# Weight sums on GpSimd and its own DMA queue, and a down projection that begins beside the third chunk, in a streaming encoder layer

## The chip, the cores and the metric

One core of a Trainium2 chip runs the whole layer in one launch. The metric is the device time of one execution in microseconds (us), and a kernel's time is the median of its timed runs. The engines of the core are named as in the profile: PE is TensorE, DVE is VectorE, ACT is ScalarE, POOL is GpSimd, SP is SyncE, which in this kernel only issues DMAs.

## The reference, cut to what matters

One layer (DEPTH 1, D 1024) acts on 1024 prompt frames and 32 sample frames, 1056 tokens that share the weights.

```python
h = rms_norm(x, g_mix); z = h @ w_in
q, k, v, ch, cb, cc, ga, gb = jnp.split(z, SPLITS, axis=-1)
a = attn_core(q, k, v) @ w_attn_out      # 16 heads of 64, window of 128, sink
u = cc * ch                              # then a causal convolution of width 3 over the frames
bo = (cb * conv) @ w_conv_out
x = x + (jax.nn.sigmoid(ga) * a + jax.nn.sigmoid(gb) * bo) @ w_mix_out
x = x + co @ w_co                        # co: cross-attention into 256 memory tokens
hm = rms_norm(x, g_mlp)
x = x + jnp.square(jax.nn.relu(hm @ w_up)) @ w_down   # w_up 1024 x 4096, w_down 4096 x 1024
```

A final RMSNorm gives the outputs. All is float32.

## The kernel before, in words

**Tiling.** Activations lie with their features on the 128 partitions and their tokens along the free dimension, in three chunks of 384, 384 and 288 tokens (`CH`), the last 32 of which are the sample. A feature block is 128 features, so x has 8 blocks of each chunk. A product of float32 is made of three matmuls in fp32r: each operand x is split into hi (a rounded copy) and lo = x - hi, and hi·hi, hi·lo and lo·hi are accumulated (`gemm` L166 to L173, `part` L1358 to L1365, `product` L1084 to L1086).

**Weights** come in tiles of 128x1024 (512 KB). `fetch_w` (L131) issues the load on SP's queue into one of two `wr` tiles. `issue_w` (L136) splits it: ScalarE copies to `wh` (L119), VectorE subtracts into `wl` (L120), three buffers each. `next_w` keeps two weights split ahead of the one in use. The list `plan` holds the kernel's steps with their weights, and `run` emits them; within each engine a scheduler at build time then orders the instructions by its own estimates, and each engine works in that order. An instruction whose operand isn't there holds up all that stands behind it on its engine; this is also so on SP's queue, whose DMA instructions wait for the tile that they store or overwrite.

**The stages,** with the times of the profile: the first norm, K and V (to about 100 us); the attention in 36 units (`Unit`), each beside a "host", a projection for Q, for the convolution or a gate (to about 560); the gates 3 to 7, the attention's output projection, and the second half of the gates (560 to 865); convolution output, mixing and cross-attention, chunk by chunk (to 1236); the up projection (to 1505); the down projection (to 1850); and the last norm of chunk 1.

**One attention unit** (`scores` L492) makes its scores on TensorE; GpSimd copies the negated sinks into the last column of the score tile `S` (L517); VectorE finds the negated maximum `nmx` (L521); ScalarE takes the exponentials over scores and sink column together, with their sum (L526); VectorE inverts that and scales (L532); `turn` transposes on TensorE (L540). GpSimd's other work there is a part of the convolution: products at L578, L591 and L593 and small copies.

**The weight sums.** The up and down projections on chunks 0 and 1 go by a scheme of seven products on 2x2 blocks (Strassen's, in Winograd's form) instead of eight. For the down projection it needs, beside the four quarters w0 to w3 of w_down, four sums of quarters: w2+w3, w0+w2, w0+(the first), w1+(that). `sum_step` (L733 to L749) makes them in 32 pieces, each with 256 columns of all four quarters, 512 KB: load, four VectorE adds of 128x256 (L736 to L739), store to `wsum_d` in DRAM. One piece takes two steps, and a host of three chunks has three steps (`steps3`), from gate 3 on. Even pieces use a tile `ws` of 128x4x256 with one DMA each way; odd ones use four separate tiles (`acc0` to `acc2` and `wsx`) with four DMAs each way. So 160 DMAs are issued on SP.

**Up** (`up_pair` L1131) makes a pair of feature blocks of the 4096 with seven products for chunks 0 and 1, and chunk 2 plainly. Twelve pairs cover three quarters of the blocks; the first eight blocks are done plainly earlier. Their values for the down projection are stored by `hidden` (L983) as operands b11, b12, b21, b22, and the combinations n3, n1, t2, n4 of four of them each are made pair by pair. For the blocks that were done plainly the combinations have to be made afterwards: `refold` (L1004) loads four blocks of 128x384, subtracts four times on VectorE (L1013 to L1016) and stores four; that is done four times, during the pairs 2 to 5.

**Down** runs eight stages (`stages` L1430). Each has eight weight tiles; a weight serves one block of eight 384-column operands (24 matmuls) and, in the first four stages, also chunk 2 (`two`, 24 more of 288 columns). The first stage has only chunk 2. Operands are loaded and split by `load_op` and `load_h2` within one step: the split stands right behind the load. The order of the products is chunk 2 alone with w_down 2, then n4 (w_down 3), b21 (w_down 1), b11 (w_down 0), t2, n3, n1, b22 with the sums; n3 goes on in t2's accumulator, and b22 in n1's.

## Time and profile before

| | |
|---|---|
| time, median of 3 runs | 1867.37 us (1866.73 to 1873.9) |
| the profiled execution | 1866.89 us, span 1865.1 us |
| busy in the span: PE, DVE, ACT, POOL | 1783.8 (96%), 1141.1 (61%), 756.6 (41%), 393.6 us (21%) |
| matmuls | 11172 |
| mean granted clock of PE | 0.983 |
| moved by DMA | 293.36 MB, 157 GB/s on average |

The profile is of one execution. A group's row gives, after a bar, the busy time, the mean of one instruction in ns, and the idle time of the engine just before them, with what ended most of it. An instruction's row in order of time gives its start, its duration, the engine, the line, the operation, and in brackets how long the engine stood idle before it and for what. A row of the waits gives the waiter, the releaser, the sum in us, how often, and the longest. A row of the DMA issues gives the queue, how many, the size of each, and the median time in us from issue to landing. A busy PE is not always at full speed: the granted clock says how much of it the chip allowed in a stretch.

### The profile page before, as it was taken

Reading aid. Unit: us, or ns where it says so; the run is one execution under the profiler, and the core shown is the slowest. Engines: PE = TensorE matmul, PEld = TensorE weight load, DVE = VectorE, ACT = ScalarE, POOL = GpSimd, SP = SyncE. Lnnn points to the kernel's source line nnn. Section 1 sums busy time; section 2 is a strip of 40 time slices with the busy share of each in tenths; the row PEclk is TensorE's granted clock in tenths of the full one; section 3 lists DMA queues with packets and bytes.
Section 4 is the critical chain, followed back from the end, with each engine's and each line's share of the span. In section 5 each row is a group of like instructions: output and inputs, shape, how many; then the busy total and the mean of one; then the engine's idle time right before and its main releaser. Section 6 shows DMA issues by size and latency. Waiting matters only on the chain. (4 is left out here: it accounts for less than half of the span.)

```text
span 1865.1 us, 30056 instructions
## 1 busy us (share of the span) xinstructions
PE 1783.8 (96%) x11172; PEld 1759.0 (94%) x11172; DVE 1141.1 (61%) x2203; ACT 756.6 (41%) x1486; POOL 393.6 (21%) x405
## 2 busy tenths in 40 slices
PE   7999999999999787899999989999999989999997
PEld 7999999999999787899999989998999989999997
DVE  7766767757656443434666677776776564445664
ACT  7643435334344100223455655642222253333453
POOL 3211010201100000001424142275455400001011
PEclk9999999999999998999999989999999999999998
DMA  4411111212238777614765657764554385444673
GB/s 182 138 64 57 61 55 60 73 51 70 69 95 250 202 231 225 215 62 133 238 239 184 227 199 251 240 212 158 177 172 132 115 272 171 167 134 147 205 248 113
DMA packets 167842, 293.36 MB, mean 157 GB/s; under 512 B 18160, under 2 KB 129552, under 8 KB 167568
## 3 DMA queue, kind: packets, MB, share of 16 engines
q1 hardware_dynamic: 167696, 291.44, 48.4%
q8 instruction: 88, 1.44, 0.3%
q14 instruction: 58, 0.48, 0.1%
HBM read 217.89 MB, written 73.48 MB: 156 GB/s over the span
## 5 line engine op out<-in xcount | busy, mean ns | idle before, releaser
L171 PE MATMUL acc<-X,wh 128*128 128x384 f32 (+1 forms) x1200 | 391.9, 327 | 16.6 <-DVE Gb L621 8.1
L172 PE MATMUL acc<-X,wh 128*128 128x384 f32 (+1 forms) x1200 | 388.4, 324 | 1.5 <-DVE X L246 1.5
L173 PE MATMUL acc<-X,wl 128*128 128x384 f32 (+1 forms) x1200 | 387.3, 323 | 0.2 <-DVE wl L120 0.2
L119 ACT CAST wh<-wr 128x1024 fp32r<-128x1024 f32 x208 | 218.2, 1049 | 405.4 <-PE acc L172 208.9
L120 DVE TENSOR_TENSOR wl<-wr,wh 128x1024 fp32r<-128x1024 f32 x208 | 276.6, 1330 | 115.4 <-ACT wh L119 114.3
L171 PEld LDWEIGHTS acc<-X,wh 128*128 128x128 f32 x1200 | 226.7, 189 | 19.0 <-ACT wh L119 7.0
L171 PE MATMUL acc<-Y,wh 128*128 128x384 f32 (+1 forms) x624 | 207.2, 332 | 26.7 <-DVE ct L706 20.9
L172 PEld LDWEIGHTS acc<-X,wh 128*128 128x128 f32 x1200 | 227.3, 189 | 2.8 <-DVE X L246 2.2
L173 PEld LDWEIGHTS acc<-X,wl 128*128 128x128 f32 x1200 | 227.1, 189 | 0.8 <-DVE wl L120 0.8
L173 PE MATMUL acc<-Y,wl 128*128 128x384 f32 (+1 forms) x624 | 205.1, 329 | 1.0 <-DMA wl<-wl_d 1.0
L172 PE MATMUL acc<-Y,wh 128*128 128x384 f32 (+1 forms) x624 | 205.0, 329 | 0.0
L171 PEld LDWEIGHTS acc<-Y,wh 128*128 128x128 f32 x624 | 120.0, 193 | 31.3 <-DVE ct L706 15.6
L242 POOL TENSOR_TENSOR xacc<-xacc,ct 128x384 f32<-128x384 f32 (+1 forms) x62 | 78.9, 1274 | 317.9 <-ACT ct L240 312.6
L173 PEld LDWEIGHTS acc<-Y,wl 128*128 128x128 f32 x624 | 120.2, 193 | 1.2 <-DMA wl<-wl_d 1.2
L172 PEld LDWEIGHTS acc<-Y,wh 128*128 128x128 f32 x624 | 120.1, 192 | 0.0
L1363 PE MATMUL acc<-Y,wh 128*128 128x384 f32 (+1 forms) x352 | 113.8, 323 | 2.2 <-ACT wh L119 2.2
L1365 PE MATMUL acc<-Y,wl 128*128 128x384 f32 (+1 forms) x352 | 113.8, 323 | 1.4 <-DVE wl L120 1.4
L1364 PE MATMUL acc<-Y,wh 128*128 128x384 f32 (+1 forms) x352 | 113.7, 323 | 0.0
L796 POOL TENSOR_TENSOR ct<-ct,ct 128x384 f32<-128x384 f32 (+1 forms) x21 | 26.9, 1283 | 408.6 <-DVE ct L795 369.4
L119 ACT CAST PTh<-pt 128x512 fp32r<-128x512 f32 (+3 forms) x94 | 46.3, 517 | 129.8 <-PE pt L540 122.3
L120 DVE TENSOR_TENSOR Y<-ct,Y 128x384 fp32r<-128x384 f32 (+1 forms) x128 | 65.8, 547 | 27.6 <-ACT Y L119 27.4
L119 ACT CAST Y<-ct 128x384 fp32r<-128x384 f32 (+1 forms) x128 | 58.3, 486 | 50.1 <-DMA ct<-ao_d 13.8
(314 smaller groups left out, 4112.7 us busy)
## 6 DMA issues: line engine op xcount, KB each, us to landing
wr<-in_w_in SPq DMA_DIRECT2D x50, 512.0 KB, 3.3
wr<-in_w_up SPq DMA_DIRECT2D x48, 512.0 KB, 4.4
wr<-in_w_down SPq DMA_DIRECT2D x32, 512.0 KB, 3.4
wr<-wsum_d SPq DMA_DIRECT2D x32, 512.0 KB, 3.8
wl<-wl_d SPq DMA_DIRECT2D x28, 512.0 KB, 4.6
wr<-in_w_conv_out SPq DMA_DIRECT2D x24, 512.0 KB, 4.2
wr<-in_w_mix SPq DMA_DIRECT2D x24, 512.0 KB, 4.4
ct<-b_d SPq DMA_DIRECT2D x64, 192.0 KB, 4.1
```

The costliest lines, as they stand in the source:

```text
L119: act.copy(hi, src)
L120: dve.tensor_sub(lo, src, hi.bitcast(F32))
L171: pe.matmul(out, wh[:, a], hi, start=(k == 0), stop=False)
L172: pe.matmul(out, wh[:, a], lo, start=False, stop=False)
L173: pe.matmul(out, wl[:, a], hi, start=False, stop=(k == len(acts) - 1))
L242: pool_e.tensor_tensor(acc, acc, sq, op=ALU.add)
L796: (dve if f == NF - 1 else pool_e).tensor_tensor(t, t, t1, op=ALU.add)
L1363: pe.matmul(a, wh[:, s], hi, start=(start and k == 0), stop=False, skip_group_check=True)
L1364: pe.matmul(a, wh[:, s], lo, start=False, stop=False, skip_group_check=True)
L1365: pe.matmul(a, wl[:, s], hi, start=False, stop=(stop and k == len(acts) - 1), skip_group_check=True)
```

## The change

1. **Weight sums.** The adds and the DMAs of a piece are GpSimd instructions: `pool_e.dma_start` issues them on GpSimd's own queue, and `pool_e.tensor_tensor` adds. `w_down` and `wsum_d` are laid out so that a piece is contiguous (rows of 4 KB in each partition); in return a weight tile of the down projection is read in four rows of 1 KB for each partition. A new tile `xacc` of 128x1056 takes the place of `acc0` to `acc2` and `wsx`: the odd pieces use it whole, the sums of squares use its three parts, and the up stage's `r` lies in it too. One step now loads the next piece and then finishes the one before (four adds, a store), and a host has two steps.
2. **Stores later.** `hidden` and the stores of n3, t2, n1, n4 in `up_pair` go through `put` into a list, and `flush` issues that list one product later.
3. **Refold moved.** The four refolds leave the up stage and stand in the first stage of down, in tiles of their own (`fold`).
4. **Another order of down.** It begins with b11 and w_down 0 beside chunk 2, then b21 (w_down 1), n4 (w_down 3), t2 with w_sum 0, whose steps alternate with chunk 2's rest (w_down 2), then n3, n1, b22. n3 starts an accumulator of its own, so t2's is added to x1 by itself, with the opposite sign for one block: eight more VectorE adds.
5. **Loads a step ahead.** `pump(n)` first splits what the last call loaded and then issues the next n loads; `pace` spreads them over a stage.

The diff, cut:

```diff
-    wsum_d = dram.tile([4, 4, 2, P, 1024], F32, name="wsum_d")
+    wsum_d = dram.tile([4, 2, 4, P, 4, 256], F32, name="wsum_d")
...
+        if name in ("w_down", "w_sum"):
+            q, j, t = at
+            return (wsum_d if name == "w_sum" else io[name])[j, t, :, :, q].rearrange("i p c -> p i c")
...
+    def xacc_tile():
+        xacc[0] = tp.tile([P, 1056], F32, tag="xacc", name=nm("xacc"))
+        return xacc[0]
...
-            accs[c] = [tp.tile([P, n], F32, tag=f"acc{c}", name=nm("xacc"))]
+            accs[c] = [xacc[0][:, CH[c][0] : CH[c][0] + n]]
...
+    def sum_tile(n):
         if n % 2:
-            new = [tp.tile([P, CH[c][1]], F32, tag=f"acc{c}", name=nm("ws"))[:, :256] for c in range(3)]
-            return None, new + [W["pool"].tile([P, 256], F32, tag="wsx", name=nm("wsx"))]
+            return xacc_tile()[:, :1024].rearrange("p (q c) -> p q c", q=4)
+        return W["pool"].tile([P, 4, 256], F32, tag="ws", name=nm("ws"))
...
     def sum_step():
-        if "new" in W:
-            at, all4, t = W.pop("new")
-            dve.tensor_add(t[3], t[2], t[3])
-            dve.tensor_add(t[2], t[0], t[2])
-            dve.tensor_add(t[0], t[0], t[3])
-            dve.tensor_add(t[1], t[1], t[0])
-            W["made"] = at, all4, t
-            return
-        if "made" in W:
-            at, all4, t = W.pop("made")
-            sum_dma(False, all4, t, quarters(wsum_d, *at))
+        old = W.pop("new", None)
         if pieces:
             at = pieces.pop(0)
-            all4, t = sum_tiles(len(pieces))
-            sum_dma(True, all4, t, quarters(io["w_down"], *at))
-            W["new"] = at, all4, t
-    steps3 = [(c, sum_step) for c in range(3)]
+            t = sum_tile(len(pieces))
+            pool_e.dma_start(t, io["w_down"][at])
+            W["new"] = at, t
+        if old:
+            at, t = old
+            for to, x, y in ((3, 2, 3), (2, 0, 2), (0, 0, 3), (1, 1, 0)):
+                pool_e.tensor_tensor(t[:, to], t[:, x], t[:, y], op=ALU.add)
+            pool_e.dma_start(wsum_d[at], t)
+    steps3 = [(c, sum_step) for c in (0, 2)]
...
+    def put(*args):
+        later.append(args)
+    def flush():
+        for args in later:
+            sp.dma_start(*args)
+        later.clear()
     def hidden(c, j, h):
-        sp.dma_start(hid2_d[:, half, i] if c == 2 else op_d[f"b{half + 1}{c + 1}"][:, i], h)
+        put(hid2_d[:, half, i] if c == 2 else op_d[f"b{half + 1}{c + 1}"][:, i], h)
...
+    def pump(n):
+        for into, at, t, get in coming:
+            into[at] = (get(), get())
+            split(*into[at], t)
+        coming.clear()
+        for into, at, src, cols, get in wanted[:n]:
+            t = tmp(cols)
+            sp.dma_start(t, src)
+            coming.append((into, at, t, get))
+        del wanted[:n]
...
+    def refold(step):
+        if step % 2 == 0:
+            if fold:
+                for to, k in (("n3", "b22"), ("n1", "b12"), ("t2", "b11"), ("n4", "b21")):
+                    sp.dma_start(op_d[to][:, step // 2 - 1], fold[k])
+            if step < 8:
+                for k in ("b12", "b22", "b11", "b21"):
+                    fold[k] = H["pool"].tile([P, 384], F32, tag="fold", bufs=4, name=nm("fold"))
+                    sp.dma_start(fold[k], op_d[k][:, step // 2])
+        else:
+            for to, x, y in (("b22", "b12", "b22"), ("b12", "b11", "b12"), ("b11", "b11", "b22"), ("b21", "b21", "b11")):
+                dve.tensor_sub(fold[to], fold[x], fold[y])
...
+    def beside_two(w, kind, then, half, f, begin, more=(), each=None):
...
+            def fn(ws, j=j, t=t, n=n):
+                prod(kind, j, t, then)(ws)
+                pump(pace(13 - 2 * n))
+                if each:
+                    each(n)
+                two(half, j, t, f, begin)(ws)
+                pump(pace(12 - 2 * n))
+            item(fn, ("w_down", w, j, t))
...
+    want(twos(0, 1), ops("b21"))
+    beside_two(0, "b11", ((*C12, True, False), (*C21, False, False), (*C22, False, False), (*C11, True, False)), 0, 0, True,
+               twos(1, 0), refold)
+    item(lambda: refold(8))
+    want(twos(1, 1), ops("n4"))
+    beside_two(1, "b21", ((*C11, True, True),), 1, 0, False)
+    want(ops("t2"))
+    beside_two(3, "n4", ((*C21, True, False),), 1, 4, True, twos(0, 0))
...
```

**Where the instructions stand.** Three places, as the builds of before and of the change order them. A row is an instruction with its line, its output and inputs, the shape, and in brackets the counters it waits for; an xN at the end stands for equal rows that follow each other.

GpSimd in the attention, between the sink copies of two neighbouring units; `Ga` are convolution products, `R` the row of norms. Before:

```order
L517 COPY S_1824<-nsink 128x4 [waits DVE_49,PE_49,Activation_49]
L578 TENSOR_TENSOR Ga_297_1729<-Ga_297_1729,R_390 128x384 [waits DVE_49]
L578 TENSOR_TENSOR Ga_299_1757<-Ga_299_1757,R_594 128x384 [waits DVE_49]
L517 COPY S_1970<-nsink 128x4 [waits PE_49,Activation_49]
L578 TENSOR_TENSOR Ga_307_1803<-Ga_307_1803,R_786 128x288 [waits DVE_49]
```

With the change, from the same copy on (`in_w_down` is the weight in DRAM, and the lines have moved by ten):

```order
L527 COPY S_1824<-nsink 128x4 [waits DVE_49,PE_49,Activation_49]
L745 DMA wsum_d<-xacc_7567 128x1024 [waits Pool_49]
L739 DMA xacc_7671<-in_w_down 128x1024 [waits DMASW3_49]
L744 TENSOR_TENSOR xacc_7671<-xacc_7671 128x256 [waits DMASW4_49]
L744 TENSOR_TENSOR xacc_7671<-xacc_7671 128x256 [waits Pool_49] x3
L588 TENSOR_TENSOR Ga_297_1729<-Ga_297_1729,R_390 128x384 [waits DVE_49]
L745 DMA wsum_d<-xacc_7671 128x1024 [waits Pool_49]
L588 TENSOR_TENSOR Ga_299_1757<-Ga_299_1757,R_594 128x384 [waits DVE_49]
L527 COPY S_1970<-nsink 128x4 [waits PE_49,Activation_49]
L739 DMA xacc_7775<-in_w_down 128x1024 [waits DMASW5_49]
L588 TENSOR_TENSOR Ga_307_1803<-Ga_307_1803,R_786 128x288 [waits DVE_49]
```

All 16 pieces that use `xacc` now stand in the first part of GpSimd's program, between its first instruction and the sink copy of the tenth unit; the 16 pieces that use `ws` stand behind the attention, where their pool is opened. The next piece's load waits for the store of the one before, since they share the tile.

SP among the attention output's weights. Before:

```order
L133 DMA wr_6890<-in_w_attn_out 128x1024
L731 DMA wsum_d<-wsx_7068 128x256
L731 DMA wsum_d<-ws_7067 128x256
L731 DMA wsum_d<-ws_6984 128x4x256
L731 DMA wsum_d<-ws_7065 128x256
L731 DMA wsum_d<-ws_7066 128x256
L731 DMA ws_7208<-in_w_down 128x256
L731 DMA wsx_7209<-in_w_down 128x256
L731 DMA ws_7137<-in_w_down 128x4x256
```

With the change (`m_d` is where the gated attention output is spilled):

```order
L137 DMA wr_6873<-in_w_attn_out 128x1024
L137 DMA wr_7013<-in_w_attn_out 128x1024
L137 DMA wr_7117<-in_w_attn_out 128x1024
L137 DMA wr_7221<-in_w_attn_out 128x1024
L137 DMA wr_7325<-in_w_attn_out 128x1024
L717 DMA m_d_83<-ct_7148 128x384
L717 DMA m_d_84<-ct_7183 128x384
L717 DMA m_d_85<-ct_7211 128x288
L137 DMA wr_7429<-in_w_attn_out 128x1024
```

The loads and stores of the sums are gone from between the weights. VectorE's adds of the same stretch have gone likewise: nothing of `ws` is left in its row.

VectorE in the up stage, in a pair during which before refolds (`ct_1396x` are the refold's tiles; `lt` are the pair's products, `wl` a weight's low part). Before:

```order
L993 SCALAR_TENSOR_TENSOR ct_13936<-pa_13911,R_13110 128x288
L1013 TENSOR_TENSOR ct_13966<-ct_13964,ct_13966 128x384
L1159 TENSOR_TENSOR lt_13877<-acc_13811,ct_13824 128x384
L1014 TENSOR_TENSOR ct_13964<-ct_13968,ct_13964 128x384
L1103 SCALAR_TENSOR_TENSOR lt_13877<-lt_13877 128x384
L120 TENSOR_TENSOR wl_13901<-s_2588_13867,wh_13900 128x1024
L1015 TENSOR_TENSOR ct_13968<-ct_13968,ct_13966 128x384
L1164 TENSOR_TENSOR lt_13880<-lt_13877,lt_13850 128x384
L120 TENSOR_TENSOR wl_2603_13942<-wr_2581_13803,wh_2602_13941 128x1024
L1016 TENSOR_TENSOR ct_13970<-ct_13970,ct_13968 128x384
L1166 TENSOR_TENSOR lt_13881<-r_13663,lt_13880 128x384
L1173 TENSOR_TENSOR lt_13904<-acc_13810,s_2558_13649 128x384
```

With the change:

```order
L1000 SCALAR_TENSOR_TENSOR ct_13785<-pa_13758,R_12960 128x288
L1145 TENSOR_TENSOR lt_13726<-acc_13660,ct_13673 128x384
L1089 SCALAR_TENSOR_TENSOR lt_13726<-lt_13726 128x384
L120 TENSOR_TENSOR wl_13750<-s_2533_13716,wh_13749 128x1024
L1150 TENSOR_TENSOR lt_13729<-lt_13726,lt_13699 128x384
L120 TENSOR_TENSOR wl_2548_13791<-wr_2526_13652,wh_2547_13790 128x1024
L1152 TENSOR_TENSOR lt_13730<-xacc_8850,lt_13729 128x384
L1159 TENSOR_TENSOR lt_13753<-acc_13659,s_2504_13498 128x384
```

The four subtractions of the refold have left VectorE's row; between them stood the last steps of the pair, of which L1173 reads out an accumulator.

189 lines of the change are left out of this document (77 added, 112 removed).

## The prediction

> **What bounds the kernel now.** The profiled execution took 1866.89 us (span 1865.1 and 1.8 around it), half a microsecond below the median of 1867.37; the sum is made against 1866.89. I read the busy table by stretches first. Columns: stretch, its length, busy us and instruction count of PE, PEld, DVE, ACT, POOL, then the granted clock, DMA share, GB/s.
>
> ```profile
> core 0: us, PE busy (x) PEld busy (x) DVE busy (x) ACT busy (x) POOL busy (x), PEclk, DMA share, GB/s
> 0.00:100.00 100.00, 88.09 (x598) 85.72 (x599) 74.64 (x144) 71.70 (x158) 29.24 (x34) 0.97 0.45 155
> 100.00:550.00 450.00, 450.00 (x2916) 443.56 (x2915) 301.03 (x792) 193.74 (x472) 57.40 (x120) 1.00 0.20 64
> 550.00:800.00 250.00, 216.16 (x1259) 210.61 (x1258) 116.89 (x252) 53.26 (x98) 0.00 (x0) 0.95 0.75 218
> 800.00:1050.00 250.00, 249.55 (x1507) 248.21 (x1506) 132.34 (x218) 109.92 (x189) 68.48 (x52) 1.00 0.54 178
> 1050.00:1230.00 180.00, 171.59 (x1114) 166.84 (x1113) 134.25 (x252) 107.25 (x217) 55.63 (x55) 0.97 0.68 232
> 1230.00:1500.00 270.00, 260.41 (x1622) 258.83 (x1620) 181.32 (x221) 69.02 (x90) 149.85 (x120) 0.99 0.48 157
> 1500.00:1550.00 50.00, 44.36 (x289) 42.95 (x290) 36.24 (x64) 28.93 (x57) 2.35 (x2) 0.97 0.88 285
> 1550.00:1850.00 300.00, 299.53 (x1857) 298.91 (x1856) 159.51 (x250) 119.94 (x203) 27.75 (x20) 1.00 0.51 167
> 1850.00:1866.00 16.00, 4.07 (x24) 3.40 (x22) 4.89 (x15) 2.81 (x7) 2.90 (x3) 0.64 0.26 98
> ```
>
> TensorE bounds the kernel, and the change takes no matmul away: only its idle time and its lost clock can be won. The largest piece is 550 to 800, where the gates and the attention projection run beside the weight sums: 250 - 216.16 = 33.8 us idle, and a clock of 0.95, which is 0.05 x 250 = 12.5 us more, 46.3 in all. From 800 on the gates and their loads go on without sums, and TensorE is busy all but 0.45 us at full clock. Next I asked the same stretch for its waits, TensorE's and then VectorE's (waiter, releaser: us in all, times, longest).
>
> ```profile
> PE acc L171 <- DVE ct L706: 20.9, 11, 4.2
> PE acc L171 <- DVE Gb L621: 12.8, 7, 4.7
> DVE ws L736 <- DMA ws<-in_w_down: 64.9, 12, 8.7
> DVE wsx L736 <- DMA wsx<-in_w_down: 19.4, 4, 5.9
> DVE Y L120 <- ACT Y L119: 12.8, 9, 2.5
> ```
>
> TensorE waits for VectorE to empty accumulators (20.9 + 12.8 = 33.7, the whole idle time); VectorE, in order, stands before an add whose weights have not landed (64.9 + 19.4 = 84.3 us). It is the wait that blocks, not the 128 adds themselves, which are (busy, count):
>
> ```profile
> 550.00:800.00 250.00, 51.53 (x128) 0.95 0.75 218
> ```
>
> **The sums, in 550 to 800.** The adds, their waits and 160 DMA issues leave VectorE and SP; GpSimd had no instruction there (0.00). What held TensorE is gone, and by the row 800 to 1050 a stage with such loads needs nothing. I leave 3 us for what comes late next (the splits of the loaded operands, whose 12.8 us of waiting stay): **-43**; bounds -46 and -33, were those 12.8 to reach TensorE in full.
>
> **The sums, at the start.** Only 16 pieces stay there. The other 16 use the new tile that is free from the beginning, and the order puts them on GpSimd between the first instruction and about 203 us, ten of them between these sink copies:
>
> ```profile
> 82.21 1.14 POOL L517 COPY S<-nsink 128x4 f32<-128x4 f32 x2 [13.91 <-PE acc L182]
> 131.65 0.20 POOL L517 COPY S<-nsink 128x4 f32<-128x4 f32 x1 [4.31 <-PE pt L540]
> 203.48 0.19 POOL L517 COPY S<-nsink 128x4 f32<-128x4 f32 x1 [14.62 <-ACT PTh L119]
> 137.42 0.51 ACT L526 ACTIVATE S<-S,nmx 128x257 f32<-128x257 f32 x1 [0.41 <-DVE nmx L521]
> 139.31 0.19 ACT L526 ACTIVATION_READ_ACCUMULATOR S<-S,nmx 128x1 f32 x1
> 144.73 1.03 PE L540 MATMUL pt<-ident,S 128*128 128x128 f32 x8
> L532 DVE TENSOR_SCALAR S<-S,rec 128x256 f32<-128x256 f32 x116 | 37.2, 382 | 1.1
> ```
>
> This is the added wait. GpSimd is in order too, so a sink copy or a convolution product now stands behind a landing. Behind the copy wait the exponentials, the scaling, and TensorE's transposes, whose place among the matmuls doesn't move. The cover of one unit: copy done 131.85, exponential 137.42, so 5.6 us; exponentials done 139.50, four scalings (1.5) and the reciprocal (about 0.2), transposes at 144.73, so 3.5 more; about 9 us.
>
> One piece takes P: a load, four adds, a store, each after the other, since one tile holds it. No DMA from GpSimd is in this trace, so P is bounded by SP's DMAs of 512 KB (us to landing, from the issue) and by GpSimd's products of 128x256:
>
> ```profile
> wr<-in_w_in SPq DMA_DIRECT2D x31, 512.0 KB, 3.3
> ws<-in_w_down SPq DMA_DIRECT2D x16, 512.0 KB, 6.0
> wl_d<-wl SPq DMA_DIRECT2D x14, 512.0 KB, 3.0
> wsum_d<-ws SPq DMA_DIRECT2D x16, 512.0 KB, 4.1
> L593 POOL TENSOR_TENSOR ct<-ct,R 128x256 f32<-128x256 f32 x8 | 5.9, 742 | 29.9 <-DVE rec L530 28.5 <-DVE ct L591 1.0 <-issue 0.5
> L359 POOL TENSOR_TENSOR macc<-macc,ct 128x256 f32<-128x256 f32 x7 | 7.8, 1109 | 3.5 <-ACT ct L357 3.2
> ```
>
> Low: 3.3 + 3.0 + 4 x 0.742 = 9.3. High: 6.0 + 4.1 + 4 x 1.109 = 14.5. I take 12: this stretch's DMA share is only 0.20, so landings near 3.3 and 3.0, one microsecond more on each for a queue written in software, and adds of 0.9. Ten pieces and about 8 us of GpSimd's own work (57.4 of 450 us is 15 in these 121; half of it stands between a load and its add in the order) have 203.5 - 82.2 + 9 = 130 us. So the stall is 10P - 122: nothing at 9.3, nothing at 12, 23 at 14.5. That treats the pieces as evenly spread; they bunch, and six stand ahead of 82 us, so that GpSimd is late already. Followed row by row with the same durations I estimate 9 us at 12, and put **+6**, with 0 and 30 as bounds. The extra adds also slow VectorE (below, a split beside GpSimd's adds takes 2.31 instead of 1.22), which has 67% of this stretch and room for it.
>
> In the Trainium skill, "DMA: Bandwidth & Descriptors", section "Anatomy of one DMA — SWDGE (gpsimd) path", a DMA from GpSimd is put at 2.0 us and its bytes at 436 GB/s. That would be 3.2 us for each of the two, P near 10, no stall, and a sum 6 us lower; no run here shows it yet.
>
> At the very start the first piece is loaded ahead of the input, and its adds stand before GpSimd's squares.
>
> ```profile
> 4.01 1.91 SPq L731 DMA_DIRECT2D ws<-in_w_down  x3
> 9.15 1.23 POOL L299 TENSOR_TENSOR sum<-raw 128x384 f32<-128x384 f32 x1 [7.81 <-DMA raw<-in_x]
> ```
>
> Three quarters of such a piece were there before, from 4.01; the squares can slip from 9.15 to about 12, and their consumer stands one instruction later on VectorE: **+1**, 0 to 4.
>
> **Refolding and late stores in the up stage** (1230 to 1500: 9.6 us idle, 0.01 x 270 = 2.7 of clock, 12.3). Ahead of one of its two longest stalls VectorE's row of work reads:
>
> ```profile
> 1285.85 0.56 DVE L1013 TENSOR_TENSOR ct<-ct,ct 128x384 f32<-128x384 f32 x1 [3.08 <-DMA ct<-b_d]
> 1287.62 0.56 DVE L1014 TENSOR_TENSOR ct<-ct,ct 128x384 f32<-128x384 f32 x1 [0.75 <-DMA ct<-b_d]
> 1288.57 1.22 DVE L120 TENSOR_TENSOR wl<-s,wh 128x1024 fp32r<-128x1024 f32 x1
> 1291.75 2.31 DVE L120 TENSOR_TENSOR wl<-wr,wh 128x1024 fp32r<-128x1024 f32 x1
> 1297.38 0.44 PE L1084 MATMUL acc<-M,wh 128*128 128x384 f32 x1 [3.27 <-DVE lt L1173]
> PE acc L1084 <- DVE lt L1173: 5.3, 2, 3.3
> ```
>
> The four subtractions of a refold wait 3.08 + 0.75 us for loads and take 4 x 0.56; TensorE then lacks the accumulator that L1173 reads. With the refold moved this goes: 5.3 idle and the 2.7 of clock, 8 at most. I take **-6** (0 to -9), as VectorE's queue stays long there. SP's deferred stores unblock the weights behind them; that hides under the same stalls.
>
> **The down stage.** It had 5.6 us idle and 0.03 x 50 of clock at its head (7.1), and 0.47 in the rest. Most of the head was one weight per 24 short matmuls:
>
> ```profile
> PE acc L1363 <- ACT wh L119: 2.2, 1, 2.2
> PE acc L1365 <- DVE wl L120: 2.1, 3, 0.7
> ```
>
> With P1 beside chunk 2 a weight serves 48, so 4.3 us and a part of the clock go: **-4**, 0 to -7. The price comes in the first 8 steps: b21 (3.1 MB), 16 blocks of chunk 2 (2.4), four refolds (6.3), eight weights (4.2), 16 MB. At 300 us for 1857 matmuls its 384 take 62 us, so 258 GB/s, less than the 285 of the head's row, with loads a step ahead. The weights are now read in rows of 1 KB, four to a partition; the 6.0 us landing above was of such reads, against 3.3, and SP fetches two weights ahead, 14 us. Eight more VectorE adds (0.56 each) hide. **+1**, 0 to 10.
>
> Sum: 1 + 6 - 43 - 6 - 4 + 1 = -45, so 1866.9 - 45 = **1822 us**.
>
> **Rivals.** *GpSimd is late by more* (P of 13.5 to 15.5): the stall is 13 to 33 and the time 1829 to 1849. For it: the chain is serial and the landings under a busy queue are 6.0; against: the low DMA share.
>
> *Slower:* a piece takes so long that attention pays for the sums. All other terms give -51, so it decides at 10P - 122 = 51, P = 17.3; at P = 19 the stall is 68 and the time 1884. It needs landings of about 7 us each. For it: no DMA of GpSimd is in the trace, and it shares VectorE's access, as the 2.31 shows. The Trainium skill has a rule to that end: "SBUF — State Buffer", section "SBUF: two separate sides", says that descriptors of GpSimd's DMAs can't be written while VectorE runs a two-port fast mode. Against: VectorE's likeliest such operation here, L532, takes 382 ns for 256 columns, hardly less than an add of that size, which has two inputs:
>
> ```profile
> L737 DVE TENSOR_TENSOR ws<-ws 128x256 f32<-128x256 f32 x16 | 6.8, 423 | 0.3
> ```
>
> *The down stage pays:* refold stores wait for VectorE, and everything behind them on SP, weights too, comes late: 10 to 25 us, 1831 to 1846. Against: the 14 us of weights ahead.
>
> *The sums' stage keeps its stalls,* because the DMA engines (0.75) bind it and not the queue: half the pieces stay, so half of 46 stays, and the time is about 1845; where nearly all stays, 1863. Against: 84 us of VectorE waits answer for TensorE's 33.7. The Trainium skill's section "Issuing engines are not separate DMA queues" on the DMA page would have it so: another issuing engine saves only issue time.
>
> **How the numbers follow.** Forecast 0.59 (1804 to 1830), GpSimd late 0.18, down stage 0.10, stalls kept 0.06, slower 0.07. The range, 1804 to 1855, runs from nearly all bounds at their best to the end of the late case, and leaves out the slower case and the tails. About 0.5% (9.3 us) is what a measurement here can tell from no change: faster, below 1858, has the forecast, the late and down cases and a part of the kept stalls, 0.88; same 0.05; slower 0.07.
>
> **What would show it.** TensorE in 550 to 800 busy nearly throughout at clock 1.00, with no wait on VectorE over 1 us; GpSimd's piece spacing in the early order, 12 us; waits of L550's transposes (L540 before) on VectorE or ScalarE between 80 and 210 us, 6 in sum; no 3 us stall between 1250 and 1350 minus 45; a down stage with less than 4 idle. Wrong it would be if TensorE idles over 20 us before 210, or if the sums' stage still waits for accumulators.

## The result, and the profile after

The changed kernel takes 1822.55 us (median of 4 runs, 1816.83 to 1825.76), the one before in the same session 1867.22 us. The ratio is 0.9749, with a 95% interval from 0.9717 to 0.9782. The forecast was 1822. The profiled execution took 1822.32 us (span 1820.5) against 1866.89 (1865.1).

The sum was right, but not each of its terms. Both kernels run 11172 matmuls, and from about the 350th to the 6600th in the same order, so the start of the k-th matmul in both traces says where time was won or lost (k counts the matmuls ahead of it; the rows 1 and 11172 are the first and the last):

| k-th matmul | where | before, us | after, us | shift | change of the shift |
|---|---|---|---|---|---|
| 1 | first product | 7.0 | 8.3 | +1.3 | +1.3 |
| 400 | memory keys, end of the start | 70.5 | 78.7 | +8.1 | +6.8 |
| 3700 | end of the attention | 580.7 | 588.8 | +8.1 | 0.0 |
| 4800 | gates, behind the sums | 805.1 | 765.3 | -39.8 | -47.9 |
| 7420 | start of up | 1234.5 | 1194.6 | -39.9 | -0.1 |
| 9000 | end of up | 1498.1 | 1451.6 | -46.6 | -6.7 |
| 11172 | last | 1857.1 | 1812.5 | -44.6 | +2.0 |

The busy table by stretches, of the changed kernel (columns as before: stretch, its length, busy us and count of PE, PEld, DVE, ACT, POOL, granted clock, DMA share, GB/s):

```profile
0.00:100.00 100.00, 82.01 (x545) 80.20 (x546) 78.79 (x120) 65.24 (x142) 52.21 (x65) 0.93 0.57 202
100.00:550.00 450.00, 450.00 (x2912) 443.65 (x2911) 311.44 (x808) 194.56 (x480) 107.45 (x191) 1.00 0.28 91
550.00:800.00 250.00, 250.00 (x1564) 249.70 (x1563) 86.75 (x145) 66.16 (x120) 66.20 (x90) 1.00 0.48 158
1440.00:1500.00 60.00, 54.32 (x326) 52.55 (x325) 41.93 (x76) 27.53 (x54) 5.22 (x5) 0.97 0.86 276
```

The stretch of the sums has no idle time and no half clock left (216.16 and 0.95 before). The attention is busy throughout although GpSimd does nearly twice the work there. The start has got worse (88.09 and 0.97 before), and 5.7 us of idle time stand where up passes into down, little less than the 6.3 in the same 60 us of the kernel before:

```profile
1490.00:1550.00 60.00, 53.69 (x348) 51.96 (x348) 40.24 (x71) 31.89 (x63) 4.51 (x4) 0.97 0.84 269
```

In 550 to 800 VectorE and SP now wait for TensorE's products and for each other's splits, hardly for landings any more:

```profile
DVE ct L716 <- PE acc L177: 66.0, 24, 3.7
SPq L137 <- DVE wl L120: 113.5, 20, 12.3
```

In the last row SP has the next weight's load ready and waits for a buffer to come free (21.2 us before).

GpSimd's own DMAs, of which the trace of before had none (KB each, median us from issue to landing), and one piece in the attention in GpSimd's order of time:

```profile
xacc<-in_w_down POOLq DMA_DIRECT2D x16, 512.0 KB, 4.1
wsum_d<-xacc POOLq DMA_DIRECT2D x16, 512.0 KB, 3.1
ws<-in_w_down POOLq DMA_DIRECT2D x16, 512.0 KB, 3.6
wsum_d<-ws POOLq DMA_DIRECT2D x16, 512.0 KB, 2.9
...
```

```profile
103.85 0.53 POOL L739 DMA_DIRECT2D xacc<-in_w_down  x1 [2.37 <-DMA wsum_d<-xacc]
107.45 3.29 POOL L744 TENSOR_TENSOR xacc<-xacc 128x256 f32<-128x256 f32 x4 [3.07 <-DMA xacc<-in_w_down]
...
111.15 0.58 POOL L745 DMA_DIRECT2D wsum_d<-xacc  x1 [0.41 <-POOL xacc L744]
...
211.33 0.53 POOL L739 DMA_DIRECT2D xacc<-in_w_down  x1 [2.80 <-DMA wsum_d<-xacc]
```

From the load at 103.85 to that at 211.33 nine pieces are made, so one follows the other after (211.33 - 103.85) / 9 = 11.9 us. The chain of one piece, with the medians of the rows above and four adds of 0.74, is 4.1 + 3.1 + 4 x 0.74 = 10.2 us; the rest is GpSimd's other work and waits between. The forecast's P, which is the chain alone, was 12.

### The profile page after: what moved, and what is told of

The parts are those of the page before. It is cut to its first block, busy times and chain, and to the rows that moved or that the text cites. A ratio compares the mean times of both kernels' runs of the same rounds, so it can differ in the third digit from the quotient of the medians.

```text
span 1820.5 us, 29893 instructions
## 1 busy us (share of the span) xinstructions
PE 1769.7 (97%) x11172; PEld 1750.3 (96%) x11172; DVE 1110.2 (61%) x2083; ACT 757.0 (42%) x1486; POOL 531.4 (29%) x597
## 5 line engine op out<-in xcount | busy, mean ns | idle before, releaser
L175 PE MATMUL acc<-X,wh 128*128 128x384 f32 (+1 forms) x1200 | 392.1, 327 | 11.3 <-ACT wh L119 8.3
L175 PE MATMUL acc<-Y,wh 128*128 128x384 f32 (+1 forms) x624 | 202.4, 325 | 0.7 <-DVE ct L1000 0.4
L177 PE MATMUL acc<-Y,wl 128*128 128x384 f32 (+1 forms) x624 | 201.9, 324 | 0.0
L176 PE MATMUL acc<-Y,wh 128*128 128x384 f32 (+1 forms) x624 | 201.7, 323 | 0.0
L175 PEld LDWEIGHTS acc<-Y,wh 128*128 128x128 f32 x624 | 117.0, 188 | 1.4 <-DVE ct L1000 0.6
L176 PEld LDWEIGHTS acc<-Y,wh 128*128 128x128 f32 x624 | 117.1, 188 | 0.0
L1363 PE MATMUL acc<-Y,wh 128*128 128x384 f32 (+1 forms) x352 | 113.2, 322 | 1.3 <-DVE lt L1145 0.7
L1364 PE MATMUL acc<-Y,wh 128*128 128x384 f32 (+1 forms) x352 | 113.3, 322 | 0.6 <-DVE Y L120 0.6
L1365 PE MATMUL acc<-Y,wl 128*128 128x384 f32 (+1 forms) x352 | 113.0, 321 | 0.0
L1004 POOL TENSOR_TENSOR ct<-ct 128x288 f32<-128x288 f32 (+1 forms) x48 | 44.8, 934 | 120.3 <-DVE ct L1000 49.8
```

What stands on the lines that cost most here:

```text
L175: pe.matmul(out, wh[:, a], hi, start=(k == 0), stop=False)
L176: pe.matmul(out, wh[:, a], lo, start=False, stop=False)
L177: pe.matmul(out, wl[:, a], hi, start=False, stop=(k == len(acts) - 1))
L1004: pool_e.tensor_tensor(h, t, t, op=ALU.mult)
L1363: pe.matmul(a, wh[:, s], hi, start=(start and k == 0), stop=False, skip_group_check=True)
L1364: pe.matmul(a, wh[:, s], lo, start=False, stop=False, skip_group_check=True)
```

## The experiments

Three questions were open: which part of the first edit frees the sums' stage, what the start pays for, and which edits matter in up and down. My theory for the first was the prediction's sentence that VectorE's wait for landings is what blocks. Shifts below are those of the k-th matmul, as in the table.

### The sums' stage: adds, DMAs, both

Both on GpSimd, in the kernel before with its tiles and steps:

```diff
-            sp.dma_start(*((x, y) if load else (y, x)))
+            pool_e.dma_start(*((x, y) if load else (y, x)))
...
-            dve.tensor_add(t[3], t[2], t[3])
-            dve.tensor_add(t[2], t[0], t[2])
-            dve.tensor_add(t[0], t[0], t[3])
-            dve.tensor_add(t[1], t[1], t[0])
+            for to, x, y in ((3, 2, 3), (2, 0, 2), (0, 0, 3), (1, 1, 0)):
+                pool_e.tensor_tensor(t[to], t[x], t[y], op=ALU.add)
```

> The kernel before with the adds and all 160 DMAs of the sums on GpSimd, its tiles, its three steps and its layout kept; all 32 pieces stay in the stage of the gates. Theory (VectorE's stand before an add whose weights have not landed is what holds TensorE): TensorE is busy throughout 550 to 800, 45 to 49 us less, 1818 to 1823, with nothing lost at the start. Rival (the DMA engines' load in that stage binds it, and the change won because half the pieces went to the attention): at least half of the 48 us stays, 1840 or more.

Only the adds (the second part of that diff):

> The kernel before with the 128 adds on GpSimd and the 160 DMAs left on SP. Theory (VectorE's wait): nearly all of the gain, 40 to 48 us, 1819 to 1827; what may be left is stores on SP that wait for GpSimd and hold the weights behind them. Rival (SP's queue: the sums' stores and loads hold back the weights): no more than 10 us, 1857 or more.

Only the 160 DMAs (the first part):

> The kernel before with the 160 DMAs of the sums on GpSimd's queue and the 128 adds left on VectorE. Theory (VectorE's wait): VectorE still stands before the same adds, so no more than 10 us of the 48, 1857 to 1875. Rival (SP's queue): nearly all of the gain, 1820 to 1830.

Adds and stores on GpSimd, loads on SP (`(sp if load else pool_e).dma_start`):

> The kernel before with the adds and the 80 stores of the sums on GpSimd, the 80 loads left on SP. Theory (whatever shares an in-order queue with the sums stands still with them: a load on SP waits until the store has freed its tile, and the weights wait behind it): at least 15 us of the stage's 48 stay, 1835 to 1865. Rival (only the stores, which wait for adds, hold up SP): the stage is as with both on GpSimd, 1820 to 1835.

Measured, with the time that TensorE lost between the 3700th and the 4800th matmul (before: 48.9; the change: 1.0):

| kernel | median, us | ratio, 95% interval | lost in the stage |
|---|---|---|---|
| b_both | 1833.44 | 0.9792 [0.9752, 0.9832] | 3.2 |
| b_dma | 1857.54 | 0.9946 [0.9928, 0.9964] | 40.6 |
| b_split | 1858.71 | 0.9964 [0.9946, 0.9983] | 39.1 |
| b_adds | 1880.42 | 1.0064 [1.0042, 1.0086] | 60.7 |

The lost time, here and below, is the sum of the distances between the starts of neighbouring matmuls, less the usual distance for their size (173.5 ns for 384 columns, 132 for 288); idle time and half clock are both in it (other sizes go by their medians in the same way).

My theory fell in the form in which I stated it. With the adds gone from VectorE but SP still carrying the DMAs, the kernel is slower than before. Its stretch of the sums:

```profile
550.00:800.00 250.00, 204.77 (x1208) 201.24 (x1207) 67.51 (x103) 43.09 (x77) 95.73 (x125) 0.92 0.71 205
```

The waits of b_adds there show why, SP's first, then ScalarE's, then TensorE's:

```profile
SPq L731 <- DMA wsum_d<-ws: 39.7, 33, 3.9
SPq L731 <- POOL ws L737: 32.8, 41, 3.4
SPq L731 <- POOL wsx L737: 27.5, 13, 6.6
...
ACT wh L119 <- DMA wr<-in_w_attn_out: 79.4, 6, 16.7
ACT wh L119 <- DMA wr<-in_w_in: 44.7, 3, 15.3
...
PE acc L171 <- DVE Ga L621: 27.3, 1, 27.3
```

SP stands before stores whose adds are not made (32.8 + 27.5) and before loads whose tile is still being stored (39.7). The weights behind them come late, 79.4 + 44.7 us of ScalarE's waits. In the kernel before these two ScalarE rows are missing, and TensorE's waits name VectorE alone. But SP's own rows, which the forecast did not look at, show it standing there too:

```profile
SPq L731 <- DMA wsum_d<-ws: 30.7, 24, 4.3
...
SPq L731 <- DVE ws L738: 12.6, 11, 5.7
SPq L731 <- DVE ws L739: 12.5, 11, 4.8
```

All rows of L731 come to 96.5 us there, and to 116.6 in b_adds. Some of that increase is b_adds's own: GpSimd's adds take 0.77 to 0.85 us there, VectorE's took 0.42, and SP stands 60.3 us before unfinished adds instead of 38.7. In b_dma the old wait is there again, undiminished:

```profile
PE acc L171 <- DVE ct L706: 19.7, 7, 4.2
...
DVE ws L736 <- DMA ws<-in_w_down: 101.7, 14, 10.7
```

The 10 us that b_dma gains are the most that the theory allowed it. b_split, expected to keep at least 15 of the 48 us, left SP only the loads, and SP stood before them all the same, for tiles that were still being stored:

```profile
SPq L731 <- DMA wsum_d<-ws: 72.7, 32, 6.6
SPq L731 <- DMA wsum_d<-wsx: 55.1, 11, 7.6
...
ACT wh L119 <- DMA wr<-in_w_attn_out: 64.9, 5, 15.4
```

So load, add and store are one chain, and each in-order row that holds a link of it stands still with it. Of the four arrangements tried only the one in which all three leave both VectorE's and SP's row frees the stage; b_both and the change have that in common. It also settles the rival that the DMA engines bind: up to its 4800th matmul, at 757.8 us, b_both keeps them as busy as the kernel before did (0.74 and 223 GB/s against 0.75 and 218), and TensorE is busy at full clock all but 2 us:

```profile
550.00:758.00 208.00, 205.99 (x1283) 205.79 (x1282) 85.95 (x125) 51.92 (x96) 146.72 (x223) 1.00 0.74 223
```

### What half of the pieces in the attention buys

The first profile of b_both took 1820.58, but its three other executions about 1833. So its median lies between what the theory (1818 to 1823) and the rival (1840 or more) had said, and it was run again.

> The kernel before with the sums' adds and DMAs on GpSimd once more, since three of its four times were 1833 and the profiled one 1820.6. Theory (nothing of the program differs between its executions, the higher times are the spread of that chip): median 1820 to 1826. Rival (the chain of 32 pieces is late in most executions, and the profiled one was an exception): median 1830 to 1835 again, and a profile at that time has over 10 us of waits that the first one lacks.

The median was 1834.51 (1827.06 to 1840.09), ratio 0.983 [0.9795, 0.9864], so the rival's time held. The profiled execution was the 1840.09 one, 19.5 us longer than the first profile: 4.4 by the 400th matmul, 1.2 in the stage of the sums, 8.2 from the 4800th to the 5600th, the rest in small pieces behind. Its stretch behind the sums, and the waits there, GpSimd's, ScalarE's and TensorE's:

```profile
763.00:911.00 148.00, 140.57 (x807) 138.89 (x806) 72.66 (x86) 43.62 (x69) 57.75 (x63) 0.97 0.59 192
```

```profile
POOL ws L737 <- DMA ws<-in_w_down: 23.3, 5, 6.7
...
ACT M L119 <- POOL ct L794: 16.5, 7, 7.0
...
PE acc L171 <- DVE Ga L621: 3.8, 1, 3.8
PE acc L171 <- ACT M L119: 1.6, 1, 1.6
```

With all 32 pieces in one stage the last sum has landed at 903 us in this execution, and in the changed kernel at 730. From the 4800th to the 5600th matmul TensorE loses 14.0 us, against 5.8 in the first profile of b_both and 0.9 in the kernel before and in the change. Two places make that up. GpSimd's additions for the mixing (L794) stand behind the last pieces; the waits of 1.6 and 0.6 us for the mixing's operand `M` that follow from it are in both profiles of b_both, and with the half clock behind them cost 4.6 and 5.3 us. The wait of 3.8 us is in the second profile alone, and with its half clock it is 6.6 of the 8.2 us between the two. VectorE's readout (L621) stands there behind three splits that take 1.64 us each beside GpSimd's adds; just before, the same split took 0.46:

```profile
761.03 0.46 DVE L120 TENSOR_TENSOR Y<-ct,Y 128x288 fp32r<-128x288 f32 x1 [2.38 <-ACT Y L119]
...
763.63 4.93 DVE L120 TENSOR_TENSOR Y<-ct,Y 128x288 fp32r<-128x288 f32 x3
768.48 1.38 DVE L621 TENSOR_TENSOR Ga<-acc,R 128x384 f32<-128x384 f32 x3
```

So GpSimd's being late, which I had priced in the attention, is real, but in the stage behind the sums, and the change avoids it there by making half of them early. Why the splits fell beside the adds in one execution and not in the other these traces don't show.

### The start

The first xacc piece tied to the norm row of chunk 2, so that no piece stands before that row (66.1 us in its own trace):

```diff
+            if len(pieces) == 31:
+                pool_e.tensor_copy(t[:, 0, 0:1], R[2][:, 0:1])
             pool_e.dma_start(t, io["w_down"][at])
```

> The change, with its first xacc piece tied to the norm row of chunk 2 (made at about 73 us in the changed kernel's profile), so that no piece stands in GpSimd's row before it. Theory (the 8.1 us that TensorE loses before 79 us come from the pieces in the start, by VectorE's gain splits beside GpSimd's adds, 5.47 us for seven instead of 2.85, and by the input's load beside the first piece): the start is back at the time of before, every later matmul is 8 earlier, about 1814 to 1816. Rival (the attention pays for a piece wherever it stands, since GpSimd is in order): the pieces now reach to about 270 us and TensorE loses in 80 to 270 what it wins before 80; 1820 to 1826.

Measured: 1815.38 us (1813.90 to 1820.39), ratio 0.9716 [0.9689, 0.9743]. The theory held in its time. The 400th matmul starts at 68.4, 2.1 ahead of the kernel before; up to the 600th (100.6, before 100.4), where its first pieces now stand, TensorE loses 2.4 us more than in the kernel before, and from there to the end of the attention 1.3 more: 6.6 of the 8.1 are won (the rest: 1.5 us behind the kernel before at the 3700th). Single executions differ, but by less than this: the 3700th matmul starts at 581.7 to 583.7 in the three traces with the tie (x_late and two below), at 588.3 to 588.8 in the four that keep early pieces with their adds (the change and three below), and at 579.0 to 583.5 in the six that start as the kernel before. To tell the adds from the DMAs, the adds were left out.

> The change without the adds of the sixteen xacc pieces and of the very last piece; their loads and stores stay at their places, so half of the sums are missing from the output. Theory (the start pays because VectorE's gain splits beside GpSimd's adds take 0.78 us instead of 0.41, and GpSimd's own steps stand behind the adds): the seven gain splits take about 2.9 us, TensorE is 1 to 3 us behind the kernel before at 70 us instead of 8, 1815 to 1819. Rival (the pieces' DMAs hold back the input and the first weights): TensorE is still 6 to 8 us behind at 70 us, 1820 to 1824.

The kernel that ran leaves out the adds of the other sixteen pieces, in `ws`, so it says nothing on the start. It took 1821.51 us, as the change does, with the stage of the sums unchanged at 1.0 lost: the adds of `ws` cost nothing there. The one that leaves out the adds in `xacc`:

```diff
-            for to, x, y in ((3, 2, 3), (2, 0, 2), (0, 0, 3), (1, 1, 0)):
+            for to, x, y in ((3, 2, 3), (2, 0, 2), (0, 0, 3), (1, 1, 0)) if len(pieces) % 2 else ():
```

> The change without the adds of the sixteen xacc pieces (half of the sums are missing from the output); their loads and stores stay, and the order packs them a little closer. Theory (the start pays because VectorE's gain splits beside GpSimd's adds take 0.78 us instead of 0.41, and GpSimd's own steps stand behind the adds): the seven gain splits take about 2.9 us, TensorE is 1 to 3 us behind the kernel before at the matmul that before started at 70.5, 1815 to 1819. Rival (the pieces' DMAs hold back the input and the first weights): TensorE is still 6 to 8 us behind there, 1820 to 1824.

The 400th matmul started at 75.0: 4.5 us behind the kernel before, where the theory said 1 to 3 and the rival 6 to 8. Its runs lie from 1816.31 to 1828.98 (median 1821.72) and decide nothing. By the traces both causes have a share, and the adds the smaller one. Of the change's 8.1 us 2.6 are there by the 290th matmul, at 55 us, and 5.5 come from the 290th to the 335th; without the adds it is 0.7 and 3.8. The first part differs as much between executions of kernels with one and the same start (0.6 ahead of the kernel before to 3.8 behind it), so nothing can be read from it. The second is 4.7 to 5.5 in the four traces with early pieces and their adds, 3.8 without the adds, and from 0.9 won to 1.6 lost in the others without early pieces: some 1 to 2 us are the adds', some 2 to 5 the DMAs' with their places in GpSimd's row, where the last of the memory's sums of squares (`macc`) ends at 66.1 us in the change, 63.5 without the adds and 59.3 in x_late. The share of the adds can be seen on VectorE's gain splits of the memory (ns: least, median, most), first before, then after, and in what TensorE then waits for in 40 to 80 of the changed kernel:

```profile
L246 DVE SCALAR_TENSOR_TENSOR raw<-raw,prm,raw x8: 471/472/475, 46.6 to 50.1; 128x256 fp32r<-128x256 f32 x8
```

```profile
L256 DVE SCALAR_TENSOR_TENSOR raw<-raw,prm,raw x8: 470/959/1108, 49.3 to 55.4; 128x256 fp32r<-128x256 f32 x8
```

```profile
PE acc L175 <- ACT ct L439: 3.0, 1, 3.0
PE pr L225 <- DVE ct L223: 1.2, 1, 1.2
```

The same instruction takes 0.96 us in the median instead of 0.47 where GpSimd adds beside it. In x_late, where it doesn't, seven of them take 2.85 us again, as before. The Trainium skill, "SBUF — State Buffer", section "SBUF: two separate sides", states that a VectorE operation with two inputs in SBUF and a GpSimd operation that reads SBUF exclude each other for a whole instruction. This trace fits that: the operation has two inputs there, and its longest, 1.11, is less than 0.47 and one GpSimd add of 0.74 together.

### Up: refold or late stores

The refolds back in the up pairs 2 to 5 (the old `refold` under `up_steps`, and `each` of the first down stage left out):

> The change with the four refolds back in the up pairs 2 to 5, as before, and out of the first down stage; the late stores stay. Theory (the refold's four subtractions, which wait for loads in VectorE's row, make the stalls of 3.4 and 2.2 us with half clock behind them): the up stage gives back 5 to 7 us, the down stage stays, 1827 to 1830. Rival (the late stores made the gain, since SP's deferred stores held the weights): within 2 us of the change, 1820 to 1825.

The stores issued at once again (`put` calls `sp.dma_start`):

> The change with the stores of hidden values and combinations issued at once, as before; the refolds stay in the down stage. Theory (refold made the gain): within 2 us of the change, 1820 to 1825. Rival (late stores made it): 5 to 7 us slower, 1827 to 1830.

Measured: a_refold 1825.91 us (ratio 0.9789 [0.9761, 0.9817]), a_noflush 1820.11 (0.9752 [0.9728, 0.9776]; the change 0.9749). The same stretch of the up stage, of the kernel before, of the change and of a_refold, and a_refold's waits in it:

```profile
1230.00:1350.00 120.00, 111.08 (x682) 109.82 (x681) 86.20 (x101) 32.03 (x44) 74.30 (x59) 0.97 0.53 173
```

```profile
1190.00:1310.00 120.00, 116.40 (x729) 115.60 (x728) 81.94 (x98) 34.09 (x46) 76.90 (x62) 0.99 0.44 144
```

```profile
1190.00:1310.00 120.00, 110.53 (x693) 109.51 (x692) 88.61 (x102) 33.20 (x44) 75.93 (x59) 0.99 0.53 176
```

```profile
PE acc L1091 <- DVE lt L1180: 5.2, 2, 3.2
```

With the refold the two waits of 3 and 2 us for the accumulator's readout are back (5.3 before), and from the 7600th to the 9000th matmul TensorE loses 8.1 us instead of 1.8. The late stores change nothing there (1.9 without them). By these traces the refold has 6.3 of the 6.7 us gained in up, and no gain of the late stores can be seen. In the first down stage, which is then free of the refolds, a_refold loses 6.6 us from the 9000th to the 9300th matmul, where the six traces with the refolds in VectorE's row there lose 8.5 to 11.3, so at least 1.9 come back. The median came out 3.4 us above the change's, under the 5 to 7 of the theory and above the rival's range; by the ratios, each against the kernel before of its session, it is 0.0040 of 1867, 7.5 us, with intervals that overlap. So the times leave the size open, and the traces carry the point.

### From up to down

In the changed kernel the longest wait of this passage is in the last up pair. VectorE's row there, with a ScalarE row ahead of it and TensorE's wait behind it:

```profile
1451.45 0.94 ACT L119 CAST Y<-ct 128x288 fp32r<-128x288 f32 x2 [3.14 <-DMA ct<-hid_d]
```

```profile
1451.91 0.97 DVE L120 TENSOR_TENSOR Y<-ct,Y 128x288 fp32r<-128x288 f32 x2 [1.58 <-ACT Y L119]
...
1455.51 0.55 DVE L1136 TENSOR_TENSOR lt<-acc,s 128x384 f32<-128x384 f32 x1
```

```profile
PE acc L1070 <- DVE lt L1136: 3.4, 1, 3.4
```

The readout of an accumulator (L1136) stands in VectorE's row behind five splits of operands for the down stage, and these wait for landings. Beginning those loads one product later, on top of x_late:

```diff
-            if last:
+            if last and what != "B11":
                 pump(4)
...
     item(open_down)
+    item(lambda: pump(4))
```

> The kernel with the first xacc piece tied to the norm row (x_late), and the operand loads of the down stage beginning one product later in the last up pair, with the last four of them behind it. Theory (in the last up pair VectorE stands before the splits of operands that land 3 to 4 us after their issue, and an accumulator's readout stands behind; 3.5 us and 3.4 us of half clock): 5 to 7 us less than x_late, 1808 to 1811. Rival (the operands are then missing at the head of the down stage instead): the same as x_late, 1813 to 1817, with a stall of some 4 us more before the first 48 matmuls of down.

Measured: 1816.09 us (1810.15 to 1819.05), ratio 0.9729 [0.9701, 0.9758], the same as x_late. The rival held: the last pair's wait stays (3.0 us, in x_late 3.5), and at the head of down TensorE waits 3.4 us for operands, where x_late's trace has 1.5 and 0.8.

Last, the refolds of the first down stage on GpSimd, with stores at once and x_late's tie:

```diff
-                    sp.dma_start(fold[k], op_d[k][:, step // 2])
+                    pool_e.dma_start(fold[k], op_d[k][:, step // 2])
...
-                dve.tensor_sub(fold[to], fold[x], fold[y])
+                pool_e.tensor_tensor(fold[to], fold[x], fold[y], op=ALU.subtract)
```

(and the fold's stores likewise.)

> The kernel with the first xacc piece tied to the norm row (x_late), the stores issued at once again, and the four refolds of the first down stage on GpSimd, adds and DMAs on its own queue, so that VectorE and SP are free of them there. Theory (the head of the down stage pays for the refold's DMAs in SP's queue and its subtractions in VectorE's row; with the refold in the up stage that head lost 2 us less): 2 to 4 us less than x_late, 1811 to 1814. Rival (the head waits for the operands' landings, which the refold does not move): the same as x_late, 1814 to 1818.

Measured: 1812.30 us (1809.62 to 1814.06), ratio 0.971 [0.9687, 0.9734]. That is the fastest version, and its median lies where the theory put it. But x_late's interval, 0.9689 to 0.9743, holds it too, and two things differ from x_late, the refold's engine and the stores, so these runs do not decide between theory and rival. From the 9000th to the 9300th matmul its trace loses 8.1 us, x_late's 11.3 and the change's 8.5; the wait in the last pair is 3.2 us still.

## Why the prediction was right or wrong, point by point

| term | predicted | measured | |
|---|---|---|---|
| sums, 550 to 800 | -43 (-46 to -33) | -47.9 | right mechanism for the change, its cause named by half; 1.9 beyond its bound |
| sums, attention | +6 (0 to 30) | 0.0 | wrong, at its bound |
| sums, start | +1 (0 to 4) | +8.1 | wrong, beyond its bound |
| up | -6 (0 to -9) | -6.7 | right; nearly all the refold's |
| down head and rest | -4 and +1 | -1.2 and +3.2 (lost to the 9300th, and behind it) | mis-sized |
| sum | -45 | -44.6 | errors of -11.6 and +12.1 cancelled |

That the time came out within a microsecond of the forecast is luck: what the stage of the sums, the attention and up gave beyond the forecast, the start and down took away. The measured column is one execution against one; the starts alone differ by some 3 us between executions. The range holds the time, though its upper end, 1855, is 6 us above the end of the late case (1849) that it is said to be.

**The sums' stage.** What held TensorE is gone entirely; the 3 us that I left for late splits did not appear. The step that failed is the sentence "It is the wait that blocks, not the 128 adds themselves", in that it takes VectorE's wait for the whole cause. Taking adds and wait out of VectorE's row (b_adds) made the kernel slower, because the same chain stood in SP's row. TensorE's waits of before name only the row that came last; SP's own would have shown the other. Whether the 51.5 us of adds would block by themselves no run shows: each run that moves the adds moves the waits with them. In the forecast this did no harm, since the change moves both. The Trainium skill's section "Issuing engines are not separate DMA queues" of "DMA: Bandwidth & Descriptors", which I had set against the change, speaks of the time to initiate a DMA. That is small here too (0.3 to 0.4 us on SP); but what is queued behind a DMA that must wait is not, and b_adds and b_both differ by 57.5 us in this stage through the issuing engine alone.

**The attention.** The chain was shorter than forecast, P of 10.2 instead of 12, and its spacing with GpSimd's other work 11.9. Still GpSimd was late: the sink copies from the third to the ninth come 11.5 to 19.6 us later than in the kernel before (115.1 against 103.6, 208.3 against 188.7), and TensorE is by then 8.1 us later itself. That leaves 3.4 to 11.5 us, and TensorE shows no wait. The step that failed is the cover, "about 9 us": it was read across two units. The copy at 131.65 is the fifth, and the exponentials at 137.42 belong to the fourth, whose copy stands at 117.42. The fifth unit's begin at 151.90, 20.1 us behind its copy:

```profile
117.42 0.19 POOL L517 COPY S<-nsink 128x4 f32<-128x4 f32 x1 [0.82 <-PE pt L540]
```

```profile
151.90 0.51 ACT L526 ACTIVATE S<-S,nmx 128x257 f32<-128x257 f32 x1 [0.66 <-DVE nmx L521]
```

(Of the first fifteen units only the ninth, the sample's, has a copy of 128x1, and the ninth group of exponentials is the single one; that fixes the pairs.) Of these units only the tenth has a short cover, 6.3 us from copy to exponentials. There ScalarE does wait for GpSimd, 2.42 us in the change:

```profile
220.56 0.41 ACT L536 ACTIVATE S<-S,nmx 128x129 f32<-128x129 f32 x1 [2.42 <-POOL S L527]
```

In x_late, where TensorE isn't late itself, it waits 5.82 us, and TensorE then 0.84 for its transposes: most of the 1.3 us that it loses beyond the kernel before from the 600th to the 3700th matmul. So the 0.0 of the change is in part a gift of the late start. The rival with P of 17.3 was not tried.

**The start.** The squares slipped to 12.15, as forecast, and up to the 290th matmul TensorE is 2.6 us behind, within the bound. The step that failed is that the term ends there: I followed the first piece only. The order puts four pieces and the load of a fifth ahead of 79 us, and what they cost is GpSimd's own steps behind landings and adds, and, for the smaller part, VectorE's gain splits at half speed. I had granted that the extra adds slow VectorE and given it room for that: this holds from 100 us on, and not at the start, where VectorE is busy 74.64 of 100 and the row of norms hangs on it. Behind the waits of 1.2 and 3.0 us the clock was 0.51 from 60.7 to 67.6; the fifteen distances between matmul starts from 62.57 to 67.54 come to 4.97 us instead of 2.60, so 2.4 us more. TensorE idles 18.0 us before 210 (11.9 before), just under the 20 that the prediction named as a sign against it.

```profile
60.70:67.60 6.90, 5.03 (x16) 5.03 (x17) 6.09 (x11) 4.07 (x14) 5.25 (x6) 0.51 0.61 218
```

**Up.** Right in place and size. The late stores, which I had put under the same stalls, show no gain.

**Down.** The head's weights are gone from TensorE's waits, as predicted: from the 9100th to the 9300th matmul TensorE loses 2.3 us instead of 7.5. But the operands have come: the term "4.3 us and a part of the clock go" left out that loads a step ahead put splits of operands that have not landed into VectorE's row in the last up pair (3.4 us of waiting), and from the 9000th to the 9100th it loses 6.2 instead of 2.3. Behind the 9300th the loss stands between the 10800th and the 11100th, 3.9 us (0.3 before), where TensorE waits for splits of operands again (0.9, 0.6 and 0.6 us); the forecast's +1 had no such term. Each of these sizes differs by some microseconds from trace to trace: x_late, with the same down stage, loses 6.0 from the 9100th to the 9300th, and 1.5 in the last place. The reads in rows of 1 KB cost nothing to speak of: w_down's weights land in 3.7 us, against 3.4 before.

## What to carry to other kernels

A chain of load, compute and store that is beside the point of a stage belongs on one engine with a queue of its own, all of it: whichever in-order row keeps one link stands still with it. The wait table of the engine that matters names only what came last, so ask every row that holds a link for its own waits, the DMA queue's too. A chain put on an idle engine is still in order with that engine's other work, so ask of every place the scheduler gives it what stands behind it, and above all of the start, where nothing is ahead of need. A cover is read from the rows of one unit, and where two units are in flight their rows stand side by side. A forecast whose sum is right is checked term by term, by the start of the same matmul in both traces.

## What the runs showed of the hardware that was not expected

GpSimd's DMAs of 512 KB landed in 4.1 and 3.6 us (loads) and 3.1 and 2.9 us (stores), about as fast as SP's (3.7 for the same weights), and most took 0.53 to 0.61 us of GpSimd to issue. The Trainium skill's section "Anatomy of one DMA — SWDGE (gpsimd) path" in "DMA: Bandwidth & Descriptors" has 2.0 us and the bytes at 436 GB/s, from which an estimate of 3.2 us follows for either; the stores agree, the loads took a little longer. The same split of VectorE's took 0.46 us alone and 1.64 beside GpSimd's adds (b_both2), the same gain split 0.47 and 0.96. The first matmul started at 7.0 to 8.4 us in most traces, but at 10.2 in a_noadd, 10.8 in b_dma and 11.5 in b_both2, where b_both, the same kernel, had 8.3: single executions differ by some 3 us at the start alone.
